# Weight buffers moved to the front of SBUF, each pair at its own offset in its tile

## The chip, the cores and the metric

The kernel runs on one core of one Trainium2 chip. The metric is the time of one execution on the device, in microseconds (us). The core has five engines, each with its own instruction queue: TensorE (PE in the profile; its loads of weights are listed apart, as PEld), VectorE (DVE), ScalarE (ACT), GpSimd (POOL) and SyncE (SP), which here issues the transfers between HBM and the on-chip memory SBUF. Matmul results go to PSUM.

## The reference

One decoder block over a sequence of 512 positions with 1,024 channels, in float32. A vector c gives shift, scale and gate for two sub-layers. The first is a mixer with two branches, a Mamba-2 scan and a pooling over several windows, each gated; the second is an MLP with a squared ReLU.

```python
mod = (jax.nn.silu(c) @ w_ada[i] + b_ada[i])[:, None, :]
shift_m, scale_m, gate_m, shift_f, scale_f, gate_f = jnp.split(mod, N_MOD, axis=-1)
h = rmsnorm(x, norm_mix_w[i]) * (1.0 + scale_m) + shift_m
x = x + gate_m * hybrid_mixer(h, ...)
h = rmsnorm(x, norm_mlp_w[i]) * (1.0 + scale_f) + shift_f
x = x + gate_f * (jnp.square(jax.nn.relu(h @ w_up[i])) @ w_down[i])
...
# in hybrid_mixer
proj = h @ w_in                       # z, xbc, dt_raw, u_pool, gate_logits
xbc = jax.nn.silu(causal_depthwise_conv(xbc, conv_w, conv_b))
y = ssd_chunked_scan(x32 * dt[..., None], dt * a_cont, bmat, cmat)
y_ssd = y.reshape(b, seq, D_INNER) @ w_branch_ssd
y_pool = causal_multiscale_pool(u_pool, pool_w, pool_scale) @ w_branch_pool
return (g_ssd * y_ssd + g_pool * y_pool) @ w_out
```

Nearly all arithmetic lies in the products with w_in (1,024 x 8,224), w_branch_ssd, w_branch_pool, w_out, w_up and w_down.

## The kernel before

Activations are held transposed: 128 channels on the partitions, the 512 positions along them. To keep float32 accuracy at the faster fp32r rate, each operand is split in two parts, `hi` (rounded to fp32r) and `lo` (the rest), and a product is three matmuls: hi x hi, hi x lo, lo x hi. This is `mm3`, lines 141 to 143; each of the three loads its own 128 x 128 weights and streams 512 columns of activations, 256 where a stage works in halves.

The weights come in units of 512 KB (128 partitions x 1,024 floats: eight blocks of 128 x 128). `load_unit` handles one: SP brings it into a raw buffer (four of them, `RAW`); ScalarE writes `hi` into a weight buffer (line 131); VectorE writes `lo = raw - hi` into another (line 132). The eight weight buffers `HL`, named hl0 to hl7 in the profile as `hl`, are handed out in a ring by `Slots`, so they go in pairs: (0, 1), (2, 3), (4, 5), (6, 7), hi in the even one. `unit` then runs eight `mm3` over the eight blocks, that is 24 matmuls into one PSUM bank. The hi and lo parts of the activations lie in the 50 buffers `s` of 128 x 512 floats.

The first 60 us compute the norms and a first group of columns by hand-ordered code (`begin` and `end`, lines 254 and 258, fill the weight buffers there with 896 columns; lines 289 and 295 are the matmuls). From 60 to about 450 us four groups of the scan alternate with units that fill TensorE's time (plain float32 matmuls at lines 427 to 519, transposes at 427 and 452). From there to the end the units of the gates, the pooled branch, w_out, w_up and w_down follow one another; the last units of w_out and w_down are done in two halves of 256 positions, those of w_out with weights split into `s` buffers. Between units, lines 156 and 157 compute the vector mod with VectorE from the adaT rows.

Tiles are placed in SBUF in the order in which they are first asked for; the 16,384 bytes of a scratch area for transfers issued by GpSimd come first. Before the change the first weight buffers are asked for in the starting loop, between `s` and raw buffers. All of `s`, raw and hl have tiles whose sizes are multiples of 2,048 bytes per partition.

```python
        HL = slots("hl", NHL, (P, 1024))
...
        hi, lo = at.get(F32R), at.get(F32R)
        act.copy(hi[:, :w], r[:, a:a + w])
        (low or dve).tensor_tensor(lo[:, :w], r[:, a:a + w], hi[:, :w].bitcast(F32), ALU.subtract)
...
        pe.matmul(ps, whi, xhi[:, t0:t1], start=start, stop=False)
        pe.matmul(ps, whi, xlo[:, t0:t1], start=False, stop=False)
        pe.matmul(ps, wlo, xhi[:, t0:t1], start=False, stop=stop)
```

Of the kernel before, what the change touches and what calls it, by code (L numbers as in the profile page):

```python
# [12 lines left out]
P = 128  # L13
T = 512
# [21 lines left out]
NSLOT, NRAW, NHL, NPU = 50, 4, 8, 3  # L36
# [22 lines left out]
def block_kernel(tc, xT, crow, arow, par, adaT, wstart, wz, wx, wpool_in, wgate, wpw, wbs, wbp, wout, wup, wdn, out):  # L59
    nc = tc.nc  # L60
    act, dve, pool, pe, sp = nc.scalar, nc.vector, nc.gpsimd, nc.tensor, nc.sync

    with (
# [3 lines left out]
    ):  # L67
        count = [0]

        def slots(name, n, shape=(P, T), where=sb):  # L70
            def make(i, dt):
                count[0] += 1
                return where.tile(list(shape), dt, tag=f"{name}{i}", name=f"{name}{i}_{count[0]}", bufs=1)
            return Slots(make, n)

        S = slots("s", NSLOT)
        XS, SZ = slots("xs", 2, (P, 4, T)), slots("sz", 2, (P, 4, T))
        MT = slots("mt", 3, (P, HG, P))
        RAW = slots("raw", NRAW, (P, 1024))
        HL = slots("hl", NHL, (P, 1024))  # L80
        SM = slots("sm", 4, (P, NC))
        SM.put(*[SM.get() for _ in range(4)])
        PU, PS = slots("ps", 8, (P, T), psp), slots("ps", 8, (P, T), psp)
# [37 lines left out]
        def load_unit(src, n=1024, low=None, at=None, cols=1024):  # L121

            at = at or HL
            with tc.high_priority() if urgent[0] else nullcontext():
# [91 lines left out]
        with tc.manual_schedule():  # L216
# [33 lines left out]
            def begin(k):  # L250

                r, hi, lo = RAW.get(), HL.get(F32R), HL.get(F32R)
                sp.dma_start(r[:, :896], wstart[k])
# [3 lines left out]
            def end(r, hi, lo):  # L257
                dve.tensor_tensor(lo[:, :896], r[:, :896], hi[:, :896].bitcast(F32), ALU.subtract)
                pool.tensor_copy(hi[:, NH:2 * NH], lo[:, :NH].bitcast(F32))
                RAW.put(r)  # L260
                HL.put(hi, lo)
                return [(hi[:, o:o + P], lo[:, o:o + P]) for o in range(0, 896, P)]
# [8 lines left out]
            first = [PS.get() for _ in range(8 - NPU)] + [PU.get() for _ in range(NPU - 1)]  # L271
# [577 lines left out]
```

## Time and profile before

| | |
|---|---|
| median of 3 runs | 992.67 us (992.05 to 994.04) |
| the profiled execution | 992.94 us, its span 991.2 us |
| mean granted TensorE clock | 0.989 |
| TensorE busy | 972.0 us, 98% of the span |
| loads of weights | 800.1 us, 81% |
| VectorE | 617.8 us, 62% |
| ScalarE | 482.9 us, 49% |
| GpSimd | 63.9 us, 6% |
| HBM read | 126.53 MB |

The profile is of one execution. Matmuls overlap each other, so the busy time and the mean duration of a matmul are not the distance between two; that is read from their starts or from how many fall in a stretch. A group of instructions is written as line, engine, operation, output<-inputs and shape, then the busy time, the mean of one in ns, and the idle time of its engine just before, with what ended most of it.

### The profile page before, as it was taken

What the parts mean: (1) busy time and instruction counts of PE and PEld (TensorE: products, weight loads), DVE (VectorE), ACT (ScalarE), POOL (GpSimd) and SP (SyncE); (2) the same over time, 40 slices, a digit from 0 to 9 for tenths busy, and PEclk for the clock granted to TensorE, in tenths of its full rate; (3) what the DMA queues carried; (4) which work ended last, traced back from release to release, by engine and by line L of the source; (5) the groups of instructions that cost most, each with busy time, mean ns of one, the idle gap of its engine ahead of it and who ended that gap; (6) DMA issues with size and microseconds to landing.
All of it is one profiled execution on the core that took longest, in us unless ns stands there. A gap on an engine that the chain in (4) does not pass through costs nothing.

```text
span 991.2 us, 12146 instructions
## 1 busy us (share of the span) xinstructions
PE 972.0 (98%) x4708; PEld 800.1 (81%) x4708; DVE 617.8 (62%) x888; ACT 482.9 (49%) x724; POOL 63.9 (6%) x71
## 2 busy tenths in 40 slices
PE   6999999999999999999999999999999999999996
PEld 4777787888788888788888888988888888888886
DVE  5987867677767776978775655654344334434443
ACT  5388879489549923553422343452233123313342
POOL 0100220110011013200000000000000000000000
PEclk7999999999999999999999999999999999999998
DMA  9836532433343232437885443032323323232302
GB/s 339 282 128 179 153 112 94 128 118 105 92 143 118 85 112 86 143 113 233 272 278 186 152 163 132 1 128 87 105 93 99 106 86 106 85 106 88 104 1 85
DMA packets 58620, 129.55 MB, mean 131 GB/s; under 512 B 4609, under 2 KB 29313, under 8 KB 58562
## 3 DMA queue, kind: packets, MB, share of 16 engines
q1 hardware_dynamic: 58562, 128.77, 40.1%
q8 instruction: 37, 0.61, 0.3%
q14 instruction: 21, 0.17, 0.1%
HBM read 126.53 MB, written 2.23 MB: 130 GB/s over the span
## 4 chain that ended last, share of the span: by engine, by line
PE 83%; ACT 7%; DVE 4%; DMA 3%; issue 2%; POOL 0%; SPq 0%; DVEq 0%; POOLq 0%; ACTq 0%
PE ps L141 25%; PE ps L142 25%; PE ps L143 25%; PE ps L295 3%; DMA mt<-cs_d 2%; PE ps L486 1%; ACT hl L131 1%; PE ps L470 1%; PE ps L466 1%; ACT L448 1%; DVE s L361 1%; DVE hl L132 1%; ACT L393 1%; ACT mt L448 1%; PE ps L185 0%
## 5 line engine op out<-in xcount | busy, mean ns | idle before, releaser
L141 PE MATMUL ps<-s,hl 128*128 128x512 f32 (+1 forms) x1272 | 491.3, 387 | 1.8 <-ACT pad L545 1.2
L142 PE MATMUL ps<-s,hl 128*128 128x512 f32 (+1 forms) x1272 | 485.4, 382 | 0.6 <-DVE s L112 0.6
L143 PE MATMUL ps<-s,hl 128*128 128x512 f32 (+1 forms) x1272 | 485.5, 382 | 0.0
L131 ACT CAST hl<-raw 128x1024 fp32r<-128x1024 f32 x153 | 160.1, 1048 | 273.9 <-PE ps L142 268.8
L141 PEld LDWEIGHTS ps<-s,hl 128*128 128x128 f32 x1272 | 239.0, 188 | 51.8 <-issue 3.7
L142 PEld LDWEIGHTS ps<-s,hl 128*128 128x128 f32 x1272 | 239.3, 188 | 48.0 <-DVE s L112 1.9
L143 PEld LDWEIGHTS ps<-s,hl 128*128 128x128 f32 x1272 | 239.2, 188 | 46.8 <-issue 0.5
L132 DVE TENSOR_TENSOR hl<-raw,hl 128x1024 fp32r<-128x1024 f32 x153 | 189.2, 1239 | 128.0 <-ACT hl L131 124.4
L679 DVE SCALAR_TENSOR_TENSOR xs<-ps,mod,xs 128x512 f32<-128x512 f32 (+1 forms) x46 | 31.3, 680 | 106.8 <-PE ps L143 106.7
L111 ACT CAST s<-sz 128x512 fp32r<-128x512 f32 x52 | 31.4, 620 | 52.9 <-DVE sz L725 42.3
L157 DVE CUSTOM_DVE_ANT_0 raw<-raw,cbc,par_t 128x1024 f32<-128x1024 f32 x32 | 40.9, 1279 | 18.4 <-DMA raw<-adaT 18.2
L112 DVE TENSOR_TENSOR s<-sz,s 128x512 fp32r<-128x512 f32 x52 | 34.9, 689 | 22.7 <-ACT s L111 22.7
L448 ACT ACTIVATE mt<-mt,ncs 128x128 f32<-128x128 f32 x128 | 41.7, 392 | 11.3 <-POOL mt L444 11.1
L361 DVE SCALAR_TENSOR_TENSOR s<-ps,par_t,s 128x511 f32<-128x511 f32 (+2 forms) x54 | 40.0, 743 | 4.5 <-ACT s L359 4.0
L295 PE MATMUL ps<-s,hl 128*128 128x512 f32 x144 | 35.6, 398 | 0.8 <-ACT s L283 0.8
L444 POOL TENSOR_SCALAR_AFFINE_SELECT mt<-mt 128x1024 f32<-128x1024 f32 x16 | 21.1, 1318 | 205.2 <-DMA mt<-cs_d 73.8
L295 PEld LDWEIGHTS ps<-s,hl 128*128 128x128 f32 x144 | 26.3, 188 | 8.6 <-ACT s L283 3.3
L365 ACT ACT_TABLE_LOAD x18 | 23.1, 1283 | 7.5 <-DVE s L361 7.3
L448 ACT ACT_TABLE_LOAD x19 | 24.4, 1283 | 0.3
L508 ACT ACTIVATE s<-sz 128x512 f32<-128x512 f32 x16 | 10.1, 630 | 27.7 <-DVE sz L507 27.5
L449 DVE TENSOR_TENSOR mt<-mt,ps 128x1024 f32<-128x1024 f32 x16 | 19.4, 1214 | 5.3 <-ACT mt L448 2.9
L111 ACT CAST s<-s 128x512 fp32r<-128x512 f32 x16 | 10.0, 622 | 25.5 <-DVE s L558 25.3
(167 smaller groups left out, 766.1 us busy)
## 6 DMA issues: line engine op xcount, KB each, us to landing
raw<-adaT SPq DMA_DIRECT2D x32, 512.0 KB, 4.3
raw<-wup SPq DMA_DIRECT2D x32, 512.0 KB, 3.2
raw<-wdn SPq DMA_DIRECT2D x32, 512.0 KB, 3.3
raw<-wx SPq DMA_DIRECT2D x18, 512.0 KB, 3.4
raw<-wz SPq DMA_DIRECT2D x16, 512.0 KB, 3.5
mt<-cs_d SPq DMA_DIRECT2D x16, 512.0 KB, 6.1
raw<-wbs SPq DMA_DIRECT2D x16, 512.0 KB, 3.2
raw<-wgate SPq DMA_DIRECT2D x16, 512.0 KB, 3.6
```

Source lines behind the costliest of these rows:

```text
L111: act.copy(hi, src)
L112: dve.tensor_tensor(lo, src, hi.bitcast(F32), ALU.subtract)
L131: act.copy(hi[:, :w], r[:, a:a + w])
L132: (low or dve).tensor_tensor(lo[:, :w], r[:, a:a + w], hi[:, :w].bitcast(F32), ALU.subtract)
L141: pe.matmul(ps, whi, xhi[:, t0:t1], start=start, stop=False)
L142: pe.matmul(ps, whi, xlo[:, t0:t1], start=False, stop=False)
L143: pe.matmul(ps, wlo, xhi[:, t0:t1], start=False, stop=stop)
L157: dve.tensor_tensor_reduce(r, r, cbc, 1.0, col("b_ada", j), ALU.mult, ALU.add, mod[:, j:j + 1])
L295: pe.matmul(first[u], w[u][i // 2], h[k][i % 2], start=k == 0 and i == 0, stop=k == 7 and i == 2)
L361: dve.scalar_tensor_tensor(t[:, sh:], ps[:, :T - sh], w(3 - sh), t[:, sh:], ALU.mult, ALU.add)
L448: act.activation(m[:, i, :], m[:, i, :], AF.Exp, bias=ncs[:, c, g * HG + i:g * HG + i + 1])
L679: dve.scalar_tensor_tensor(x, ps[:, t0:t1], mod[:, gate + j:gate + j + 1], x, ALU.mult, ALU.add)
```

## The change

The weight buffers are asked for first, before all other tiles, and then put back, so that they are handed out in the order 0 to 7 as before. Each of their tiles becomes 32 floats longer (1,056 floats, 4,224 bytes), and the buffer is a window of 1,024 floats in it. The window starts 4, 2, 24 or 28 floats into the tile, that is 16, 8, 96 or 112 bytes, for pair 0, 1, 2, 3. The scratch area for transfers issued by GpSimd shrinks from 16,384 to 1,024 bytes per partition.

```diff
-        def slots(name, n, shape=(P, T), where=sb):
+        def slots(name, n, shape=(P, T), where=sb, first=0):
             def make(i, dt):
+                i += first
                 count[0] += 1
                 return where.tile(list(shape), dt, tag=f"{name}{i}", name=f"{name}{i}_{count[0]}", bufs=1)
             return Slots(make, n)
...
-        HL = slots("hl", NHL, (P, 1024))
+        SHIFT = (4, 2, 24, 28)
+
+        def shifted(i, dt):
+
+            o = SHIFT[i // 2]
+            return slots("hl", 1, (P, 1056), first=i).get(dt)[:, o:o + 1024]
+
+        HL = Slots(shifted, NHL)
+        HL.put(*[HL.get() for _ in range(NHL)])
...
-    nc = bacc.Bacc("TRN2", target_bir_lowering=False, num_devices=1)
+    nc = bacc.Bacc("TRN2", target_bir_lowering=False, num_devices=1, dynamic_dma_scratch_size=1024)
```

## The prediction

> **What bounds the kernel now.** I read the page's busy times, slices, chain and costliest groups, then the loads of weights shape by shape, then stretches and single starts in the long steady part.
>
> ```profile
> span 991.2 us, 12146 instructions
> PE 972.0 (98%) x4708; PEld 800.1 (81%) x4708; DVE 617.8 (62%) x888; ACT 482.9 (49%) x724; POOL 63.9 (6%) x71
> PEclk7999999999999999999999999999999999999998
> ...
> PE 83%; ACT 7%; DVE 4%; DMA 3%; issue 2%; POOL 0%; SPq 0%; DVEq 0%; POOLq 0%; ACTq 0%
> ...
> L141 PE MATMUL ps<-s,hl 128*128 128x512 f32 (+1 forms) x1272 | 491.3, 387 | 1.8 <-ACT pad L545 1.2
> L142 PE MATMUL ps<-s,hl 128*128 128x512 f32 (+1 forms) x1272 | 485.4, 382 | 0.6 <-DVE s L112 0.6
> L143 PE MATMUL ps<-s,hl 128*128 128x512 f32 (+1 forms) x1272 | 485.5, 382 | 0.0
> L131 ACT CAST hl<-raw 128x1024 fp32r<-128x1024 f32 x153 | 160.1, 1048 | 273.9 <-PE ps L142 268.8
> ...
> L132 DVE TENSOR_TENSOR hl<-raw,hl 128x1024 fp32r<-128x1024 f32 x153 | 189.2, 1239 | 128.0 <-ACT hl L131 124.4
> ...
> L295 PE MATMUL ps<-s,hl 128*128 128x512 f32 x144 | 35.6, 398 | 0.8 <-ACT s L283 0.8
> ...
> L289 PE MATMUL ps<-s,hl 128*128 128x512 f32 x16 | 4.9, 389 | 0.0
> ```
>
> The reader is to see that TensorE is busy for 98% of the span at the full granted clock after the first slice, that its 3,816 matmuls of lines 141 to 143 wait for nearly nothing (1.8, 0.6 and 0.0 us), and that the two instructions that fill a weight buffer wait for TensorE (268.8 us) or for each other. Since these matmuls overlap, their mean of 382 ns is no period. The period comes from stretches and starts:
>
> ```profile
> 700.00:750.00 50.00, 50.00 (x222) 41.39 (x222) 20.50 (x23) 15.05 (x19) 0.00 (x0) 1.00 0.31 102
> 750.00:800.00 50.00, 50.00 (x222) 41.39 (x221) 20.11 (x22) 13.75 (x16) 0.00 (x0) 1.00 0.29 95
> 800.00:850.00 50.00, 50.00 (x222) 41.42 (x221) 21.72 (x26) 17.88 (x25) 0.00 (x0) 1.00 0.28 95
> 850.00:900.00 50.00, 50.00 (x223) 41.39 (x222) 19.31 (x21) 10.67 (x12) 0.00 (x0) 1.00 0.28 95
> 900.00:950.00 50.00, 50.00 (x222) 41.42 (x221) 22.88 (x27) 20.41 (x28) 0.00 (x0) 1.00 0.26 85
> ...
> 700.00:950.00 250.00, 250.00 (x1104) 207.01 (x1104) 104.51 (x117) 77.75 (x98) 0.00 (x0) 1.00 0.29 94
> ...
> 500.00:510.00 10.00, 10.00 (x46) 8.29 (x45) 8.46 (x15) 2.11 (x2) 0.00 (x0) 1.00 0.82 282
> ...
> 700.00:710.00 10.00, 10.00 (x45) 8.27 (x45) 3.95 (x4) 2.11 (x2) 0.00 (x0) 1.00 0.27 91
> ...
> 610.11 0.28 PE L143 MATMUL ps<-s,s 128*128 128x256 f32 x1
> ...
> 619.83 0.28 PE L143 MATMUL ps<-s,s 128*128 128x256 f32 x1
> ```
>
> The columns of a stretch are its length, TensorE, weight loads, VectorE, ScalarE and GpSimd (busy us and count), granted clock, DMA share and GB/s. Between 700 and 950 us one matmul of 512 columns takes 250.00 / 1104 = 0.2264 us; I use 226.5 ns. The two starts of the half-width matmuls (of the same loop, with weights held in s buffers) lie 81 matmuls apart: 9.72 / 81 = 120.0 ns. The difference, 106.5 ns for 256 columns, is 0.416 ns per column, so 512 columns cost 213.0 ns, and each matmul that loads its own weights has 13.5 ns over. That leftover is the only part of the steady state on which a place in SBUF could act. It comes with all 3,816 matmuls of the loops and the 144 + 16 of the start (lines 295 and 289): 3,976 x 13.5 ns = 54 us.
>
> **The change part by part.** It adds and removes no operation: the counts of the page should stay, transfers, waits and buffer order too, since the eight weight buffers are put back in the order 0 to 7. It moves addresses. By the tile sizes, added up in order of first use, all s and hl buffers of before start at the same place modulo 2,048 bytes; afterwards each hl tile is 4,224 bytes (33 x 128), all other tiles move by multiples of 2,048, and modulo 128 the weights lie 16, 8, 96 and 112 bytes off the activations. Four edits:
>
> *The smaller scratch area.* Every transfer of the profile is issued by SP, none by GpSimd:
>
> ```profile
> q1 hardware_dynamic: 58562, 128.77, 40.1%
> ...
> raw<-wup SPq DMA_DIRECT2D x32, 512.0 KB, 3.2
> raw<-wdn SPq DMA_DIRECT2D x32, 512.0 KB, 3.3
> ```
>
> I cost it at 0. Were each load of a unit a full 1 us later, the four raw buffers and the 268.8 us in which ScalarE waits for TensorE would cover it; without that cover, 153 x 1 us would be the ceiling, and nothing speaks for it. It has no end in the range.
>
> *The order of the tiles.* High address bits change. The five 50 us stretches run through all eight hl buffers and through 16 or more s slots, and hold 222, 222, 222, 223, 222 matmuls; the stretch with 282 GB/s of DMA and 8.46 us of VectorE holds 46 against 45. Neither which buffer, nor who else is at work, shows in the period. 0, between -1 and +1 us (half a matmul of 222 in each such stretch is 0.2%, 2 us over the span; I halve it).
>
> *ScalarE's and VectorE's writes into shifted buffers* (lines 131, 132, 254, 258). The nearest rows are the same operations on shifted and unshifted tiles:
>
> ```profile
> L361 DVE SCALAR_TENSOR_TENSOR s<-ps,par_t,s 128x511 f32<-128x511 f32 x18 | 13.4, 744 | 4.0 <-ACT s L359 4.0
> L361 DVE SCALAR_TENSOR_TENSOR s<-ps,par_t,s 128x510 f32<-128x510 f32 x18 | 13.4, 742 | 0.2
> L361 DVE SCALAR_TENSOR_TENSOR s<-ps,par_t,s 128x509 f32<-128x509 f32 x18 | 13.4, 742 | 0.3
> ...
> L282 DVE SCALAR_TENSOR_TENSOR s<-s,amod,ps 128x512 f32<-128x512 f32 x8 | 6.0, 744 | 1.2 <-PE ps L185 1.2
> ...
> L545 ACT COPY pad<-ps 128x512 f32<-128x512 f32 x8 | 4.6, 578 | 0.0
> L410 ACT COPY s<-ps 128x512 f32<-128x512 f32 x8 | 4.6, 578 | 4.7 <-PE ps L143 4.7
> ```
>
> Line 361 works 4, 8 and 12 bytes into its tile and takes 742 to 744 ns, line 282 at the start of one takes 744; line 545 writes 64 bytes into a tile, line 410 at the start, both 578. So 0. The bound: ScalarE's and VectorE's hl instructions are 1.2% and 0.7% of the chain, 19 us; 2 parts in 744, the largest spread of these rows, is 0.05 us either way.
>
> *TensorE reading weights at another offset than the activations.* No row shows fp32r weights there; all weight blocks of before are 512 bytes apart and aligned with their activations. The nearest rows are the leftover itself. From below: all of it goes, -54 us. From above: it doubles everywhere, +54 us. Of the two reading rates the loads tell more:
>
> ```profile
> L142 PEld LDWEIGHTS ps<-s,hl 128*128 128x128 f32 x1272 | 239.3, 188 | 48.0 <-DVE s L112 1.9 <-issue 1.7
> ...
> L486 PEld LDWEIGHTS ps<-mt,s 128*64 128x64 f32 x256 | 13.7, 136 | 9.8 <-issue 6.1 <-PE ps L466 2.3 <-DVE mt L449 0.9
> ```
>
> 64 columns more cost 52 ns, 0.81 ns a column: the weights are read half as fast as the moving operand (0.416). While 128 weight columns are read, 256 moving columns pass, so the distance between the two reading places grows by 128 columns, 512 bytes, in every load. A shift of 2 to 28 columns only changes where this sweep begins. An interference that depends on the distance is then met equally often, and one that does not depend on it stays. So I take 0 and keep -54 and +54 as the ends.
>
> **The sum.** 0 + 0 + 0 + 0 on the profiled execution's 992.9 us (span 991.2), which is 0.3 us over the median 992.67 of the three runs. I put 992.7.
>
> **The rivals.**
> *The leftover is a quarrel over SBUF between weights and activations, and the shifts part them.*
>
> ```profile
> 700.50 0.39 PE L141 MATMUL ps<-s,hl 128*128 128x512 f32 x1
> 700.50 0.19 PEld L142 LDWEIGHTS ps<-s,hl 128*128 128x128 f32 x1
> 700.72 0.39 PE L142 MATMUL ps<-s,hl 128*128 128x512 f32 x1
> ```
>
> For it: each load starts with the matmul ahead of it, both on aligned addresses, and the leftover stays the same through stretches of different DMA and VectorE load, so its cause lies within TensorE's own reads and not with the others. Against it: the two rates. All gone gives 939 us; halfway, or two pairs of four, -27 us, 966 us. Units would then come faster, but fills keep pace: one fill holds ScalarE 1.05 and VectorE 1.24 us in a unit of 24 x 226.5 ns = 5.4 us.
> The Trainium skill, page "TensorE: Matmul & The Clock Gate", section "Wait — 56ns, not 53.3ns?", has warm back-to-back matmuls start N / 2.4 GHz plus about 2.5 ns apart, an estimated 215.8 ns for 512 columns. By that page this rival's far end would be 992.9 - 3,976 x 10.7 ns = 950 us; the trace's 226.5 ns disagrees with the page, and no run here shows yet what the rest is.
> *The pair 8 bytes in straddles.* Of the four shifts only 8 bytes is no multiple of 16. If weights are fetched in groups of four columns, each group of that pair takes two accesses, and its loads cost another leftover: 3,976 / 4 = 994 loads x 13.5 ns = +13.4 us, 1,006 us. It decides as soon as such a load holds its matmul back by over 2 ns (994 x 2 ns = 2 us). For it: the load above ends at 700.69 us and the next matmul starts at 700.72, so a load has only 0.03 us to grow into. Against it: line 361 pays nothing at 8 bytes. If all four shifts cost it, the time is 1,046 us.
> The Trainium skill, page "SBUF — State Buffer", gives SBUF lines of 16 bytes, with a penalty for each cross to a new line; that is this second rival's rule, and no row of before tests it for weights.
> *The shift does not arrive:* the compiler could place tiles otherwise; then the time is 992.7 as well.
>
> **How the numbers follow.** A measurement of this kernel (992.05 to 994.04) tells about 0.2%, 2 us, from no change. No effect, or a shift that does not arrive: 0.48, within 990.7 to 994.7. The first rival: 0.34, from 939 to 990, two thirds of it above 966, since the two rates speak against a full release. The second: 0.18, from 995 to 1,046, mostly below 1,006. Reaching down to 966 and up to 1,006 leaves about 0.11 below and 0.05 above. The likeliest case's own range is 991 to 994.5.
>
> **What would show it.** Right: the same counts, 222 matmuls in 50 us, loads of 188 ns, 120 ns between half-width starts. The first rival: over 225 in 50 us, alike in all pairs or by pair, in runs of 24 matmuls. The second: a quarter of the units with fewer matmuls per us and loads longer than 188 ns. Fills of line 131 or 132 off 1,048 and 1,239 ns would show the third edit wrong; TensorE waiting for hl, the order. My prediction fails if the period depends on the place of the weights below 128 bytes: then the sweep argument is the wrong step.

## The result, and the profile after

The change makes the kernel slower: 1,008.95 us median of 4 runs (1,008.54 to 1,010.40) against 993.15 us (992.05 to 994.04) for the kernel before, a ratio of 1.0162 [1.0145, 1.0180]. The profiled execution took 1,010.40 us, its span is 1,008.7 us, 17.5 us more than the 991.2 of before. Lines 131, 132, 141 to 143 and 295 of before are 140, 141, 150 to 152 and 304 now. Of the runs below, one execution of f1 (4,135 us) and one of g2 (1,979 us) took a multiple of their kernel's other times and are left out of the ratio of f1 and the time of g2.

From the page of the changed kernel, the busy times, the granted clock and the costliest groups:

```profile
span 1008.7 us, 12146 instructions
PE 990.1 (98%) x4708; PEld 803.2 (80%) x4708; DVE 619.5 (61%) x888; ACT 483.0 (48%) x724; POOL 67.7 (7%) x71
PEclk9999999999999999999999999999999999999998
...
L150 PE MATMUL ps<-s,hl 128*128 128x512 f32 (+1 forms) x1272 | 497.3, 391 | 1.1 <-ACT pad L554 0.6
L152 PE MATMUL ps<-s,hl 128*128 128x512 f32 (+1 forms) x1272 | 492.8, 387 | 0.0
L151 PE MATMUL ps<-s,hl 128*128 128x512 f32 (+1 forms) x1272 | 490.6, 386 | 0.3 <-DVE s L121 0.3
L140 ACT CAST hl<-raw 128x1024 fp32r<-128x1024 f32 x153 | 159.5, 1045 | 289.6 <-PE ps L151 289.1
...
L141 DVE TENSOR_TENSOR hl<-raw,hl 128x1024 fp32r<-128x1024 f32 x153 | 190.8, 1249 | 131.6 <-ACT hl L140 126.7
```

The same instructions run (12,146; 4,708 matmuls), at full granted clock. The matmuls of the loops still wait for nothing (1.1, 0.0, 0.3 us). The fills of the weight buffers are no dearer (1,045 and 1,249 ns, before 1,048 and 1,239), and ScalarE has more time on its hands, not less: its wait for TensorE before a fill grew from 268.8 to 289.1 us. So nothing arrives late. TensorE itself is slower, and the stretches show where. First before, then after; the columns are the stretch, its length, and busy time and count of TensorE, weight loads, VectorE, ScalarE and GpSimd, then clock, DMA share and GB/s.

```profile
0.00:60.00 60.00, 52.28 (x205) 39.30 (x205) 47.60 (x74) 30.06 (x46) 5.82 (x15) 0.89 0.78 278
60.00:250.00 190.00, 187.48 (x956) 150.61 (x956) 140.46 (x211) 159.57 (x260) 28.23 (x27) 1.00 0.42 126
250.00:445.00 195.00, 193.58 (x966) 156.18 (x965) 146.89 (x217) 112.34 (x167) 29.89 (x29) 1.00 0.36 112
445.00:600.00 155.00, 155.00 (x684) 127.78 (x683) 106.92 (x151) 52.00 (x69) 0.00 (x0) 1.00 0.66 213
600.00:700.00 100.00, 100.00 (x580) 88.62 (x579) 54.57 (x89) 38.20 (x65) 0.00 (x0) 1.00 0.25 83
```

```profile
0.00:60.00 60.00, 51.50 (x198) 38.62 (x198) 47.60 (x74) 29.20 (x44) 9.18 (x15) 1.00 0.77 279
60.00:250.00 190.00, 188.13 (x937) 149.21 (x938) 139.30 (x210) 157.50 (x257) 27.91 (x28) 1.00 0.42 124
250.00:445.00 195.00, 194.37 (x964) 155.32 (x963) 143.06 (x214) 111.91 (x166) 30.57 (x29) 1.00 0.36 111
445.00:600.00 155.00, 155.00 (x667) 125.35 (x666) 107.96 (x149) 52.76 (x68) 0.00 (x0) 1.00 0.62 204
600.00:700.00 100.00, 100.00 (x575) 87.43 (x574) 56.21 (x94) 38.90 (x67) 0.00 (x0) 1.00 0.29 93
700.00:950.00 250.00, 250.00 (x1076) 202.78 (x1075) 100.74 (x112) 72.52 (x91) 0.00 (x0) 1.00 0.28 94
```

TensorE is busy throughout in both and gets through fewer matmuls: 7, 19, 2, 17 and 5 fewer in these five stretches, and 1,076 against 1,104, 28 fewer, between 700 and 950 us. At 950 us the kernel is 78 matmuls behind; at 226.5 ns each that is 17.7 us, the whole of the 17.5 us of span. The loss is spread over the program. Up to 445 us the counts say less of it, since the scan's own matmuls, of other lengths, are counted with the others.

A stretch also counts the matmul that is already running at its start, so the distance between two starts is 250 / 1,103 = 226.7 ns before and 250 / 1,075 = 232.6 ns after: 5.9 ns more for every matmul of this stretch, all of which are of full width (512 columns) and load their weights from a shifted buffer. (One matmul more or less in a count is 0.2 ns.) All 3,688 full-width matmuls at this price would be 21.8 us, so some of them lose less. The matmuls of half width whose weights lie in s buffers, which did not move, are as they were. Here are two of their starts, 24 matmuls apart, from the list of instructions in order of time:

```profile
627.05 0.28 PE L150 MATMUL ps<-s,s 128*128 128x256 f32 x1
...
629.93 0.28 PE L150 MATMUL ps<-s,s 128*128 128x256 f32 x1
```

2.88 us / 24 = 120.0 ns, as before. But matmuls of half width whose weights do lie in shifted buffers became faster. In the last units of w_down 72 of them follow one another; these are the starts of the first and the last of the 72, before and then after:

```profile
962.30 0.28 PE L141 MATMUL ps<-s,hl 128*128 128x256 f32 x1
...
970.81 0.28 PE L143 MATMUL ps<-s,hl 128*128 128x256 f32 x1
```

```profile
980.28 0.28 PE L150 MATMUL ps<-s,hl 128*128 128x256 f32 x1
...
988.65 0.28 PE L152 MATMUL ps<-s,hl 128*128 128x256 f32 x1
```

The 71 distances take 8.51 us before and 8.37 us after, 119.9 and 117.9 ns. The kernel has 288 such matmuls, so this gains about 0.6 us. A load is not longer than before: 188 to 189 ns, in starts 233 ns apart.

```profile
L152 PEld LDWEIGHTS ps<-s,hl 128*128 128x128 f32 x1272 | 240.4, 189 | 52.2 <-issue 0.5
```

Nor is it one pair of buffers. A unit has 24 matmuls and the pairs take turns, so the first matmuls of five units in a row (pairs 0, 1, 2, 3, 0) give the distance for each pair:

```profile
701.11 0.40 PE L150 MATMUL ps<-s,hl 128*128 128x512 f32 x1
...
706.70 0.39 PE L150 MATMUL ps<-s,hl 128*128 128x512 f32 x1
...
712.28 0.39 PE L150 MATMUL ps<-s,hl 128*128 128x512 f32 x1
...
717.86 0.39 PE L150 MATMUL ps<-s,hl 128*128 128x512 f32 x1
...
723.45 0.40 PE L150 MATMUL ps<-s,hl 128*128 128x512 f32 x1
```

5.59, 5.58, 5.58 and 5.59 us, that is 232.5 to 232.9 ns for the pairs shifted by 16, 8, 96 and 112 bytes. Before, a unit takes 5.44 us. The loss is one quantity: the distance between the starts of two full-width matmuls. The experiments ask what sets it.

### The profile page after: what moved, and what is told of

Read it like the earlier page. It is cut to its first block, busy times and chain, and to the rows that moved or that the text cites. A ratio compares the mean times of both kernels' runs of the same rounds, so it can differ in the third digit from the quotient of the medians.

```text
span 1008.7 us, 12146 instructions
## 1 busy us (share of the span) xinstructions
PE 990.1 (98%) x4708; PEld 803.2 (80%) x4708; DVE 619.5 (61%) x888; ACT 483.0 (48%) x724; POOL 67.7 (7%) x71
## 4 chain that ended last, share of the span: by engine, by line
PE 88%; DVE 4%; ACT 4%; DMA 2%; issue 1%; POOL 1%; DVEq 0%; SPq 0%; POOLq 0%; ACTq 0%
PE ps L150 27%; PE ps L152 27%; PE ps L151 27%; PE ps L495 2%; DMA mt<-cs_d 1%; PE ps L475 1%; PE ps L479 1%; DVE sz L166 1%; DVE hl L267 1%; ACT hl L140 1%; DVE xs L166 1%; PE ps L461 1%; DVE s L291 0%; DVE s L294 0%; PE ps L194 0%
## 5 line engine op out<-in xcount | busy, mean ns | idle before, releaser
L150 PE MATMUL ps<-s,hl 128*128 128x512 f32 (+1 forms) x1272 | 497.3, 391 | 1.1 <-ACT pad L554 0.6
L152 PE MATMUL ps<-s,hl 128*128 128x512 f32 (+1 forms) x1272 | 492.8, 387 | 0.0
L151 PE MATMUL ps<-s,hl 128*128 128x512 f32 (+1 forms) x1272 | 490.6, 386 | 0.3 <-DVE s L121 0.3
L140 ACT CAST hl<-raw 128x1024 fp32r<-128x1024 f32 x153 | 159.5, 1045 | 289.6 <-PE ps L151 289.1
L141 DVE TENSOR_TENSOR hl<-raw,hl 128x1024 fp32r<-128x1024 f32 x153 | 190.8, 1249 | 131.6 <-ACT hl L140 126.7
L518 POOL TENSOR_TENSOR s<-s 128x256 f32<-128x256 f32 x16 | 17.7, 1109 | 68.6 <-ACT s L517 68.6
```

## The experiments

The expectations call the theories by letters. A: what counts is where the weights lie relative to the activations, below 128 bytes. B: it is the weight block's own start off a boundary. C: it is the place at the front of SBUF, or the tiles' stride of 4,224 bytes as such. D: hi and lo now lie an odd multiple of 128 bytes apart. E: the distance between weights and activations counts up to 512 bytes, not only up to 128. G: the distance counts, and beside it where a read starts against lines of SBUF. Each experiment shows its edit against the changed kernel ("after") or the kernel before, and its row for 700 to 950 us, from which I give the distance between starts as 250 us / (count - 1). The medians of before on the chips used lie between 992.4 and 993.2 us.

**Changing one part, or only the shifts.** e1 keeps everything of the change but the shifts; e2 keeps the shifts and the longer tiles, but leaves the buffers at their old place in the order; e3 and e4 take other shifts.

```diff
 e1, against after
-        SHIFT = (4, 2, 24, 28)
+        SHIFT = (0, 0, 0, 0)
 e2, against after
-        HL.put(*[HL.get() for _ in range(NHL)])
 e3, against after
+        SHIFT = (8, 16, 24, 32)
 e4, against after
+        SHIFT = (1, 2, 4, 12)
```

> The changed kernel with all four shifts 0: the weight buffers are still first, in tiles of 4,224 bytes, with the small scratch area; only the windows start at the tile's start. Theory A (the place of the weights relative to the activations below 128 bytes sets the period of a matmul) and theory B (a weight block that does not start on a 128-byte boundary costs more by itself): 992 to 994 us, 226.7 ns from matmul to matmul. Theory C (the place in the front of SBUF, or the distance of 4,224 bytes between buffers): about 1,009 us and 232 ns, as with the shifts.

> The four shifts alone: weight tiles of 4,224 bytes are asked for where the kernel before asks for them, between the s and raw buffers. Theories A and B: 1,007 to 1,011 us, 230 to 234 ns a matmul. Theory C: 992 to 994 us and 226.7 ns.

> As the changed kernel, with windows 32, 64, 96 and 128 bytes into the tiles, so that one trace holds four offsets. Theory A with a period of 128 bytes: pair 3 (128 bytes) at 226.7 ns, the other three at 229 to 235 ns, about 1,007 us. A period of 64 bytes: pairs 1 and 3 at 226.7 ns; of 32 bytes: all four at 226.7 ns and 993 us. Theory B with lines of 16 or 32 bytes: all four at 226.7 ns; with lines of 64 or 128 as for A.

> As the changed kernel, with windows 4, 8, 16 and 48 bytes into the tiles. Theory A: all four between 229 and 236 ns, 1,006 to 1,012 us; if the cost grows with the distance, pair 0 (4 bytes) is nearest to 226.7 ns. Theory B: a constant cost for one more line touched, the same in all four pairs.

e1: 1,004.58 us, 1.0119 [1.0102, 1.0136]. e2: 1,008.85 us, 1.0161 [1.0145, 1.0176]. One run each of e3 and e4: 1,008.43 and 1,004.21 us. The rows of e1 and e2:

```profile
700.00:950.00 250.00, 250.00 (x1083) 204.55 (x1082) 101.33 (x113) 73.89 (x93) 0.00 (x0) 1.00 0.28 95
```

```profile
700.00:950.00 250.00, 250.00 (x1076) 202.57 (x1075) 100.69 (x112) 71.89 (x91) 0.00 (x0) 1.00 0.27 95
```

e2 is the change over again (1,076 matmuls), so the front of SBUF is not needed for the loss. e3, whose shifts are all multiples of 32 bytes, costs as much as the change: no straddling of 16-byte lines is needed. And e1 is the surprise, outside what A, B and C forecast: with no shift at all, three quarters of the loss is still there, at 231.1 ns. In the trace its starts repeat, on average 226.7, 232.5 and 234.2 ns apart after the three matmuls of each `mm3`, alike in every pair. What e1 still has of the change is the front place, which e2 can do without and f1 below tests alone, and the tiles of 4,224 bytes. They are 33 x 128 bytes, and every second buffer, the lo of each pair, lies 128 bytes off a multiple of 256.

e4 gives the first sign that there is no simple price for a shift. Again the first matmuls of units in a row (pairs 1, 2, 3, 0, then 1):

```profile
703.45 0.40 PE L150 MATMUL ps<-s,hl 128*128 128x512 f32 x1
...
708.99 0.39 PE L150 MATMUL ps<-s,hl 128*128 128x512 f32 x1
...
714.43 0.40 PE L150 MATMUL ps<-s,hl 128*128 128x512 f32 x1
...
719.96 0.39 PE L150 MATMUL ps<-s,hl 128*128 128x512 f32 x1
...
725.55 0.40 PE L150 MATMUL ps<-s,hl 128*128 128x512 f32 x1
```

5.54 us (230.8 ns) at 8 bytes, 5.44 us (226.7 ns, nothing lost) at 16 bytes, 5.53 us (230.4 ns) at 48 and 5.59 us (232.9 ns) at 4, the smallest shift. Theories A and B forecast a loss in all four pairs. The changed kernel has the same 16 bytes in its pair 0, with lo 128 bytes further in both, and loses 6 ns there.

**Place and distance apart.** f1 moves the buffers to the front and shrinks the scratch area, with whole tiles of 4,096 bytes and a filler tile behind them, so that all distances stay as before modulo 2,048. f2, f3 and f4 leave the order of before and give the weight tiles 6,144 bytes with a window in them; f2 shifts only lo by 128 bytes, f3 all weights by 16, f4 all weights by 128. (To make room, their scratch area is 8,192, 512 and 512 bytes.)

```diff
 f1, against before
         HL = slots("hl", NHL, (P, 1024))
+        HL.put(*[HL.get() for _ in range(NHL)])
+        sb.tile([P, 320], F32, name="gap")
...
-num_devices=1)
+num_devices=1, dynamic_dma_scratch_size=15360)
 f2, f3, f4, against before
+        def window(i, dt):
+            o = 32 * (i % 2)        # f2; its hi tiles stay at 1024 floats;  f3: o = 4;  f4: o = 32
+            t = sb.tile([P, 1536], dt, tag=f"hl{i}", name=f"hl{i}_{count[0]}", bufs=1)
+            count[0] += 1
+            return t[:, o:o + 1024]
+        HL = Slots(window, NHL)
```

> The kernel before with its weight buffers moved to the front of SBUF, tiles of 4,096 bytes as before, and a gap of 1,280 bytes behind them, so that every weight block keeps its distance to the activations modulo 2,048 bytes (0) and hi and lo stay 4,096 bytes apart. Theory C (the front of SBUF as a place costs): about 1,004 us and 231 ns a matmul, as with all shifts 0 in the front. Theory D (hi and lo 128 bytes apart modulo 512, from the tiles of 4,224 bytes) and theory E (each block's distance to the activations below 512 bytes): 992 to 994 us, 226.7 ns.

> The kernel before with only the four lo buffers moved by 128 bytes in their place; hi buffers and all other tiles keep their distances modulo 2,048 bytes. Theory C: 992 to 994 us. Theory D: about 1,004 us, with the pattern 226.7, 232.5, 234.2 ns of the run with all shifts 0 in the front. Theory E: the hi loads stay at 226.7 ns and only the load of lo (line 143's) changes, so between 993 and 1,004 us.

> The kernel before with all eight weight buffers moved by 16 bytes in their place, so hi and lo keep their distance modulo 2,048 bytes and only the distance to the activations changes, from 0 to 16. Theories C and D: 992 to 994 us, 226.7 ns. Theory E: 230 ns or more, 1,004 us or more.

> As the run with all buffers moved by 16 bytes in place, by 128 bytes instead. Theories C and D: 992 to 994 us, 226.7 ns. Theory E: slow if the period of the distance is longer than 128 bytes (1,004 us or more), fast if it is 128 bytes or a part of it; then the distance of hi and lo cannot matter either in the run with lo alone moved.

f1: 992.99 us, 1.0005 [0.9995, 1.0014]. f2: 1,005.64 us, 1.0136 [1.0119, 1.0153]. f3: 1,009.19 us, 1.0166 [1.0146, 1.0186]. f4: 1,009.06 us, 1.0165 [1.0144, 1.0185]. Their rows, in this order:

```profile
700.00:950.00 250.00, 250.00 (x1105) 207.08 (x1103) 103.77 (x117) 77.08 (x97) 0.00 (x0) 1.00 0.29 95
```

```profile
700.00:950.00 250.00, 250.00 (x1084) 204.52 (x1083) 101.91 (x114) 74.00 (x93) 0.00 (x0) 1.00 0.29 96
```

```profile
700.00:950.00 250.00, 250.00 (x1073) 202.42 (x1072) 100.98 (x113) 72.48 (x91) 0.00 (x0) 1.00 0.29 94
```

```profile
700.00:950.00 250.00, 250.00 (x1078) 202.68 (x1077) 101.47 (x113) 72.81 (x91) 0.00 (x0) 1.00 0.29 95
```

f1 is the kernel before in another place, 1,105 matmuls: C falls. f4 shifts weights by a whole 128 bytes and loses as much as the change (232.1 ns), so a bad start below 128 bytes isn't needed, and A alone does not do; the distance counts above 128 bytes too, as E has it. f4 also has hi and lo at the same place, so D isn't needed. f2 gives e1's rate, and in the trace its starts repeat in e1's pattern, 226.7, 232.5 and 234.2 ns. That is the pattern that D forecast; E forecast one longer distance, that of lo's load, and two of three are longer, so what a load costs is not read off its own place alone. In f2 every pair lies 0 and 128 bytes off the activations; in e1 the pairs lie at 0 and 128 or at 256 and 384. That these act alike is why I read the distance modulo 256 bytes.

The trace of f3 holds one thing more. Here are the starts of two units that load from the same buffers, pair 3, and work on the same activations, those of the first norm; each time the next unit's start follows.

```profile
220.03 0.39 PE L147 MATMUL ps<-s,hl 128*128 128x512 f32 x1
...
225.47 0.39 PE L147 MATMUL ps<-s,hl 128*128 128x512 f32 x1
...
427.06 0.40 PE L147 MATMUL ps<-s,hl 128*128 128x512 f32 x1
...
432.66 0.40 PE L147 MATMUL ps<-s,hl 128*128 128x512 f32 x1
```

The first unit takes 5.44 us, 226.7 ns a matmul, as in the kernel before; the second takes 5.60 us, 233.3 ns. The addresses are the same, so the place alone does not set the price: at 16 bytes the same reads run in either of two regular states. Up to 450 us f3 goes from one to the other, with one exception, only where the scan's matmuls come between two stretches of full-width matmuls; from 455 us on it stays in the dear one. That points to what ran just before.

**Distance or the start itself.** g1 shifts weights and activations together by 16 bytes, g2 the activations alone; s buffers become windows in tiles of 2,304 bytes and hl buffers in tiles of 4,352, both multiples of 256. g3 and g4 use such hl tiles at four shifts each, with hi and lo now at the same distance.

```diff
 g1, against after
+        S = Slots(lambda i, dt: slots("s", 1, (P, 576), first=i).get(dt)[:, 4:4 + T], NSLOT)
+        SHIFT = (4, 4, 4, 4)        # tiles of (P, 1088) instead of (P, 1056)
 g2, against g1
+        SHIFT = (0, 0, 0, 0)
 g3 and g4, against after, s buffers as before
+        SHIFT = (8, 16, 40, 48)     # g3: 32, 64, 160, 192 bytes;  g4: (6, 56, 60, 63), 24, 224, 240, 252 bytes
```

> Weights in the front and all activations (the 50 s buffers) each 16 bytes into their tiles, tiles widened to a multiple of 256 bytes: the distance between the two is 0 again, while the weights' own place is the one that was slow at distance 16. Theory E (the distance between weights and activations modulo 256 bytes): 991 to 995 us, 226.7 ns. Theory B (the weights' own start off a boundary costs): about 1,009 us.

> The same with the activations alone 16 bytes into their tiles; the weights' place is that of the fast kernels (distance -16, or 240 modulo 256). Theory E: 1,002 to 1,012 us. Theory B: 992 to 995 us.

> A scan in the front with tiles of 4,352 bytes (17 x 256), hi and lo of a pair at the same distance: 32, 64, 160, 192 bytes. Theory E: each pair between 228 and 236 ns, about 1,008 us. If the 13.5 ns over the streaming time could be lowered by a place, some pair shows less than 226.7 ns.

> The same scan at 24, 224, 240 and 252 bytes. Theory E: each pair between 228 and 236 ns; 252, that is 4 bytes ahead of the activations, tells whether the smallest shift costs as much as a large one.

g1: 1,002.00 us, 1.0097 [1.0080, 1.0114]. g2: 1,005.17 us (one execution). g3: 1,008.99 us, g4: 1,000.60 us, one run each. The rows of g1 and g2, and the first matmuls of units of g4 (pairs 1, 2, 3, 0):

```profile
700.00:950.00 250.00, 250.00 (x1089) 203.63 (x1088) 102.02 (x114) 74.00 (x93) 0.00 (x0) 1.00 0.30 97
```

```profile
700.00:950.00 250.00, 250.00 (x1080) 202.90 (x1080) 100.44 (x113) 73.41 (x92) 0.00 (x0) 1.00 0.29 95
```

```profile
700.48 0.39 PE L150 MATMUL ps<-s,hl 128*128 128x512 f32 x1
...
706.08 0.40 PE L150 MATMUL ps<-s,hl 128*128 128x512 f32 x1
...
711.54 0.39 PE L150 MATMUL ps<-s,hl 128*128 128x512 f32 x1
...
716.98 0.39 PE L150 MATMUL ps<-s,hl 128*128 128x512 f32 x1
...
722.52 0.39 PE L150 MATMUL ps<-s,hl 128*128 128x512 f32 x1
```

Moving the activations by 16 bytes costs 250 / 1,079 = 231.7 ns, nearly as much as moving the weights: it takes two. But with both moved by the same 16 bytes, at distance 0, the starts are still 229.8 ns apart and the time, 1,002.00 us, is neither what E forecast (991 to 995) nor what B did (about 1,009), so the distance is not the whole of it. The place of the start counts as well, which is G. These runs do not tell whether that is the start of the weights or of the activations. In g4, weights 224 bytes ahead cost 5.60 us a unit (233.3 ns), 240 ahead 5.46 (227.5), 252 ahead, that is 4 bytes behind a multiple of 256, 5.44 (226.7), and 24 ahead 5.54 (230.8). E forecast 228 to 236 ns in all four and missed two. And 240 ahead is the same distance as in g2, modulo 256, where it costs 231.7. In g3, 32, 64 and 160 bytes give 233.3 to 233.5 ns by the same reading of its trace and 192 bytes 229.6. No pair goes below 226.7 ns.

**All tiles together, and the wide tiles.** The i kernels are before with a scratch area that is 64, 128 or 32 bytes smaller, so that every tile of SBUF moves down by as much. j1 is g1 with both windows at 0.

```diff
 i_all_tiles_32, against before (64: 16320; 128: 16256)
+num_devices=1, dynamic_dma_scratch_size=16352)
 j1, against g1
+        S = Slots(lambda i, dt: slots("s", 1, (P, 576), first=i).get(dt)[:, 0:0 + T], NSLOT)
+        SHIFT = (0, 0, 0, 0)
```

> The kernel before with nothing changed but the scratch area, 64 bytes smaller, so that every tile of the kernel lies 64 bytes lower and all distances stay. Theory E (distance between weights and activations alone): 991 to 995 us, 226.7 ns a matmul; the run with both moved by 16 bytes would then have to be slow for another reason. Theory G (the distance, and also where a read starts against lines of 128 or 256 bytes): 998 to 1,012 us.

> The same by 128 bytes. Theory E: 991 to 995 us. Theory G with lines of 128 bytes: 991 to 995 us; with lines of 256 bytes: 998 to 1,012 us.

> The kernel that moved weights and activations together by 16 bytes, with both windows back at the start of their widened tiles (4,352 and 2,304 bytes, 17 and 9 times 256); all distances of that kernel are kept, only the 16 bytes of absolute place are gone. If a start 16 bytes off a line costs by itself (the part of theory G that the runs by 64 and 128 bytes leave): 991 to 995 us, 226.7 ns. If the wider tiles cost, by the distances of 256 instead of 2,048 bytes between activations and weights: about 1,002 us, with 228.3 and 231.7 ns in turn.

> The kernel before with every tile 32 bytes lower, all distances kept. If a read must start on a line of 32 bytes or less: 991 to 995 us, 226.7 ns a matmul. If on a line of 64 bytes: 998 to 1,004 us, as with both moved by 16 bytes.

All are the kernel before: 992.87 us, 1.0001 [0.9990, 1.0012] at 64 bytes; 992.07 us, 0.9993 [0.9981, 1.0004] at 128; 991.98 us, 0.9998 [0.9986, 1.0010] at 32; j1 993.45 us, 1.0002 [0.9991, 1.0014]. The rows of the 32-byte kernel and of j1 (those at 64 and 128 bytes hold 1,105 matmuls too):

```profile
700.00:950.00 250.00, 250.00 (x1105) 207.01 (x1104) 104.54 (x117) 77.75 (x98) 0.00 (x0) 1.00 0.28 93
```

```profile
700.00:950.00 250.00, 250.00 (x1105) 207.01 (x1104) 104.57 (x117) 77.82 (x98) 0.00 (x0) 1.00 0.29 95
```

So the loss of g1 comes from its 16 bytes and not from its wider tiles. A common move by 32, 64 or 128 bytes is free and one by 16 is not: at distance 0, reads that start on any of these multiples of 32 bytes are good. G with lines of 64, 128 or 256 bytes falls; lines of 32 remain.

**Smaller elements.** h1 is before with all hi and lo parts in bf16, which leaves out precision (the products no longer have the accuracy of fp32r); h2 is h1 with all weights 128 bytes into their tiles.

```diff
 h1, against before (and the six bitcasts of hi and lo dropped)
-F32R = mybir.dt.float32r
+F32R = mybir.dt.bfloat16
 h2, against h1
+            t = sb.tile([P, 1152], dt, tag=f"hl{i}", name=f"hl{i}_{count[0]}", bufs=1)
+            return t[:, 64:64 + 1024]
```

> The kernel before with hi and lo of weights and activations in bf16 instead of fp32r (it computes at lower precision: 16 significant bits in all), at the places of before, distance 0. If the 13.5 ns over the streaming time come from TensorE's two reads of 4-byte elements, they shrink: 214 to 220 ns a matmul, 945 to 975 us. If they are a fixed price of a load of weights: 226.7 ns, about 992 us.

> The bf16 kernel with all weights moved by 128 bytes, the distance that cost 6 ns a matmul in fp32r. If the cost is a collision of two reads of 4-byte elements: within 2 us of the bf16 kernel at distance 0. If the place itself costs: 15 us more than that.

One run each: 961.04 and 961.12 us. The same kind of stretch, from 670 to 920 us, and a group of loads of h1, then the stretch of h2:

```profile
670.00:920.00 250.00, 248.79 (x1137) 113.37 (x1159) 109.10 (x122) 79.53 (x100) 0.00 (x0) 1.00 0.29 99
...
L141 PEld LDWEIGHTS <-hl 128*128 128x128 bf16 x1272 | 124.7, 98 | 139.6 <-issue 4.9 <-ACT hl L131 0.3
```

```profile
670.00:920.00 250.00, 248.79 (x1137) 113.32 (x1158) 109.20 (x122) 79.55 (x100) 0.00 (x0) 1.00 0.29 99
```

Some matmul records are missing here; the loads are complete, 1,159 and 1,158, so the starts lie 250 / 1,158 = 215.9 ns apart, with or without the 128 bytes that cost f4 5.4 ns. With 0.416 ns a column, 213.0 for 512, an estimate from the fp32r starts, the leftover is down from 13.7 to 2.9 ns. In bf16 neither the leftover of before nor the price of 128 bytes is there; other shifts were not run. More than one thing differs: the elements have two bytes instead of four, a load takes 98 ns instead of 188, and the weights are read in another pattern (in the trace 32 by 4 elements instead of 128), so the runs do not say which of these removes it.

## Why the prediction was wrong, point by point

*What bounds the kernel* was right: TensorE, waiting for nothing, and the leftover per matmul as the only part of the steady state on which a place in SBUF could act. It did act, and on nothing else.

*The smaller scratch area and the order of the tiles*, 0: right. f1 puts the buffers first with the distances kept, and gives 1.0005 [0.9995, 1.0014]; j1 does so with the scratch area of 1,024 bytes, and gives 1.0002 [0.9991, 1.0014].

*ScalarE's and VectorE's writes into shifted buffers*, 0: right. Fills measured 1,045 and 1,249 ns in the changed kernel; in f1, where the buffers are as aligned as before, the same groups show 1,048 and 1,246, so the 10 ns more of VectorE do not follow the shift:

```profile
L134 DVE TENSOR_TENSOR hl<-raw,hl 128x1024 fp32r<-128x1024 f32 x153 | 190.3, 1246 | 128.5 <-ACT hl L133 124.1 <-PE ps L468 0.4
```

*TensorE reading weights at another offset*, 0 with ends of -54 and +54 us: this step failed, and with it the sum. It measured +17.5 us of span, 5.9 ns for a full-width matmul between 700 and 950 us. The sweep argument took two mean rates, 0.81 and 0.416 ns a column, and concluded that a shift only changes where the sweep of the distance begins. That holds if both reads run at their rates whatever happens. The traces show otherwise: the starts fall into patterns that repeat with the matmuls (226.7, 232.5, 234.2 in e1 and f2; one steady 226.7 in before), and in f3 the same buffers and activations run in a state of 226.7 ns and in one of 233.3. So one regular state can be dearer than another, and an average over all phases says nothing on which of them the reads settle in. How a state is entered and held is not shown. The prediction's own last sentence on the period named this as the place where it would fail.

*The first rival* had the place right and, at full width, the sign wrong. There is a quarrel between weights and activations (f1 against f2, f3, f4 and g2), but on the same addresses modulo 256, and on a multiple of 32 bytes, it is at its smallest at full width. The rival took the leftover of 13.5 ns for the worst case because all was aligned; at full width it was the best that any fp32r kernel here reached. At half width its sign was right: the shifts shortened the distance from 119.9 to 117.9 ns, but on 288 matmuls only.

*The Trainium skill*, page "TensorE: Matmul & The Clock Gate", section "Wait — 56ns, not 53.3ns?", gave an estimated 215.8 ns for 512 columns. In bf16 the trace agrees (215.9); in fp32r it does not, with 226.7 at best and 233.2 over the stretch of f3. The page "SBUF — State Buffer" has in its section "Who interferes with whom" two read ports for TensorE, one for the moving operand and one for loads of weights, independent of each other, and says that TensorE never waits on anyone. The runs do not bear this out for fp32r at full width: moving either operand by 16 bytes against the other costs 5.0 to 6.5 ns a matmul (g2, f3), while the other engines do the same work.

*The second rival* came near in size for one pair, 1,006 us, but not in kind. All pairs lost about 6 ns, loads stayed at 188 to 189 ns, and e3 loses all of it with shifts that are multiples of 32 bytes. Its price for four pairs, 1,046 us, is far off.

*The range* took its upper end from the 8-byte pair. The end of +54 us for the unknown term was right to keep, but nearly all the weight above zero went to that one mechanism. That misalignment of any kind could cost something between 0 and 13.5 ns in all pairs was not among the cases.

Three things stay open. What the hardware does in those reads is not shown; "quarrel" is a word for the pattern. The law of the distance is not found: in g4, 4 bytes behind or 16 bytes behind a multiple of 256 cost 0 to 0.8 ns, and 32 bytes behind or ahead cost 6.6 (g4, g3), while 16 behind costs 5.0 in g2. And the same shift does not always give the same rate: 16 bytes cost nothing in pair 2 of e4 and 6 ns in pair 0 of the change, and both in f3. f3's two states suggest that what ran just before decides; no run sets that directly. Why half width gains from a shift is not known either.

No fp32r kernel here beats the kernel before.

## What to carry to other kernels

When matmuls run back to back in fp32r, each with a load of its own weights, keep the weights and the moving operand of 512 columns at the same place modulo 256 bytes and on a multiple of 32; weight tiles of an odd multiple of 128 bytes (e1) are enough to lose 1.2% of the time, with no wait to show for it. With 256 columns this place was not the best one, so measure there. Look for such a loss in the number of matmuls in a busy stretch or in the starts of a unit, since busy shares, idle times and mean durations hardly move. And where two streams share a resource, do not reason from their mean rates: ask which repeating state they settle in, and measure one shifted case.

## What the runs showed of the hardware that was not expected

- The distance between starts of fp32r matmuls of 512 columns, each with its own load, is 226.7 ns at best and goes up to 233.2 over a stretch with the place of the operands alone (f3, 250 / 1,072), at full granted clock and with loads of 188 to 189 ns.
- The same buffers, shifted by 16 bytes, and the same activations run at 226.7 ns a matmul in one unit and at 233.3 in another of the same execution (f3).
- With 256 columns the shifts of the change shorten the distance, from 119.9 to 117.9 ns.
- A common move of all tiles by 32, 64 or 128 bytes costs nothing (1,105 matmuls each); weights and activations moved together by 16 bytes cost 3.1 ns a matmul (1,089).
- Weights 4 bytes behind a multiple of 256 cost nothing (g4, 226.7 ns), 4 ahead 6.2 ns (e4, its lo at 132), 24 ahead 4.1 ns, 32 ahead 6.6 ns: it is not the size of the misalignment that sets the price.
- In bf16 the same loops run at 215.9 ns, and 128 bytes between weights and activations make no difference (h1, h2).
